# Layer 2's queries moved into the stage of sums, its near heads in one TensorE order, its weight sums in layer 1

## The chip, the cores and the metric

The kernel runs on one core of a Trainium2 chip. The metric is the device time of one execution in microseconds; the median of three runs before the change is 1518.73 us (1516.59 to 1519.83). A profile comes from one more execution, taken with the hardware profiler.

The engines are named as in the profile: PE is TensorE's matmuls, PEld its weight loads, DVE is VectorE, ACT ScalarE, POOL GpSimd, SP SyncE, which issues the DMAs here.

## The reference

A two-layer bidirectional encoder on 1024 tokens of width 1024, with 256 memory tokens. Everything is float32.

```python
h = rmsnorm(x, norm_gain[l])
# layer 1 (even): qa, ka, va, qb, kb, vb, qm, gate = split(h @ w_in_even)
ya = global_gqa(...)          # 8 heads over all tokens
yb = window_gqa(...)          # 8 heads over +-128 tokens
ym = memory_attn(qm, mk, mv)  # 4 heads over the 256 memory tokens
x = x + (concat(ya, yb, ym) * silu(gate)) @ w_out_even
# layer 2 (odd): qc, kc, vc, qm, gate = split(h @ w_in_odd)
yc = neighborhood_attn(qc, kc, vc, rpb_c)   # 16 heads, an 8 x 16 window on the token grid
ym = memory_attn(qm, mk, mv)
x = x + (concat(yc, ym) * silu(gate)) @ w_out_odd
out = rmsnorm(x, final_norm_gain)
```

The change concerns layer 2: 16 near heads (the neighbourhood attention), whose queries, keys and values are 8 tiles of 128 columns of `w_in_odd` each (two heads a tile), 4 memory heads, and 12 tiles of gates.

## The kernel before, in words

**Precision.** Each float32 operand is split in a high and a low part; a product is three matmuls (high x high, high x low, low x high) into one PSUM bank. So a tile of 128 output columns for all 1024 tokens, projected directly, is 8 blocks of the inner dimension x 3 x 2 halves of 512 tokens (`token_steps`, matmul on line 228, or line 59 where `Pinned` issues it).

**Seven products.** Some products are cut in 2 x 2 blocks and formed by seven block products in place of eight, with sums and differences of the blocks (Strassen's scheme in Winograd's form). The output projections of both layers do it (`out_project`); the sums of their weights are made by `weight_sums`, a generator with 16 units, each of a load of a [128, 4, 192] tile, four POOL operations of 128x192 and a store. And `front`, the stage of sums between the layers, does it for pairs of layer 2's input tiles: its loop goes over pairs of tiles, each with seven products of 4 x 3 matmuls (`product`, line 1413), two of which, x and z, are done early for the first five pairs, by a plan written out as a string. The results go to DRAM (`gd` for gates, `mqd` for memory queries) by `end`. Before the change the pairs are gates 8 to 11 and 0 to 5, and the four tiles of memory queries. `front` also makes the values of the first two near pairs.

**Layer 1's heads** (`even`): four `global_pair`s, each of 16 blocks of 128 queries; `side`, the weight sums of layer 1's output, takes one step before each group of two blocks, so 8 steps a pair. Then the windowed heads.

**Layer 2's heads** (`opening`, then `odd`). `opening` computes the memory heads; its TensorE instructions keep the order of the program (`Pinned`), and `fill(SLOT)` puts some 5800 columns of projection work between their parts: the first pair's queries, the values of the other six pairs, the first keys, and second queries. Then `odd` loops over the eight near pairs. `near_head` does one head: for each of 8 blocks of 128 queries the scores (lines 1023, 1024) against up to three neighbouring blocks of keys, on DVE the bias and the maximum (line 1031) and its negation (line 1034), the exponential on ACT (line 1035), the reciprocal on DVE (line 1036) and the scaling on POOL (line 1037); two blocks later the transposes (`flip`, line 122), their split into high and low part (`p_parts`, ACT line 114 and DVE line 462) and the products with the values (line 1006). At each block `pull` takes two steps of work that was put off: the next pair's keys and queries, directly projected, at the end gates 6 and 7 and the first of the output products (`begin_out`, line 1144). `side` makes the sums of layer 2's output weights here, on POOL, two steps a head. Gates 0 to 5 and 8 to 11 are loaded from DRAM and multiplied in `gated`.

`k_pair` evicts a pair of keys on ACT and DVE (line 344) and copies each head's rows to the other 64 partitions by DMA (lines 349, 350). `q_pair` evicts queries by two ACT and two DVE instructions a half (lines 326, 327).

**What sets the order.** The Tile framework simulates the program and orders each engine's instructions by it; `with self.ahead(kind)` moves instructions forward by an offset out of the table `AHEAD`; `issue_after` holds one back behind another; `keep_in_program_order` (`Pinned`) fixes the order of those that it wraps. Layer 2's row of the table:

```python
"l1": dict(first=300, sink=300, evict=300, exp=200, flip=-20, part=200, pv=-60, close=60),
```

Tiles come out of pools with a number of buffers for each name; a new tile waits until the oldest of its name is released.

## Time and profile before

| | |
|---|---|
| median of 3 runs | 1518.73 us |
| the profiled execution | 1515.65 us, its span 1513.9 us |
| granted TensorE clock, mean | 0.994 |
| layer 1's heads, about | 150 to 660 us |
| layer 1's output projection | 660 to 790 us |
| stage of sums (`front`) | 790 to 952 us |
| opening of layer 2 | 952 to 1077 us |
| near heads | 1077 to 1387 us |
| layer 2's output projection | 1387 to 1514 us |

The stages run into each other; the bounds are read from the lines that run in each.

How to read it: the page's first part has busy time, share of the span and number of instructions of each engine; the chain is the work that ended last, followed back from the last instruction. Groups of instructions name the line, the engine, the operation, the tiles (out<-in), the shapes, the count, busy us and mean ns, and then the engine's idle time before them with what ended it. A matmul's duration covers its passage through the array; the spacing of successive starts is what it costs in a stream. In the wait view each row has who waited, for whom, the us in total, the times, and the longest.

### The profile page before, as it was taken

How to read it: one execution, taken by the hardware profiler on the slowest of the kernel's cores; microseconds unless marked ns; L12 is line 12 of the kernel's file. 1: busy time of each engine (PE TensorE's matmuls, PEld its weight loads, DVE VectorE, ACT ScalarE, POOL GpSimd, SP SyncE). 2: the span in 40 equal slices, each digit the busy share in tenths (PEclk: the TensorE clock that was granted, in tenths of full speed). 3: DMA queues.
4: the chain of work that ended last, by engine and by line, in shares of the span. 5: the costliest groups of instructions: out<-in, count | busy, mean ns of one | idle time of the engine just before them, and what ended most of it. 6: DMA issues, size and time to landing. Idle time of an engine off the chain costs nothing.

```text
span 1513.9 us, 25309 instructions
## 1 busy us (share of the span) xinstructions
PE 1479.4 (98%) x8413; PEld 1281.5 (85%) x8413; DVE 1046.0 (69%) x2255; ACT 830.2 (55%) x1822; POOL 659.9 (44%) x782
## 2 busy tenths in 40 slices
PE   9999999999999999999999999999999999999997
PEld 8898898988888788787878778999788888888886
DVE  7686777767776588777578865443577777777754
ACT  8743665556655365655445544433566666666552
POOL 1323547456563545443450000131456566664355
PEclk9999999999999999999999999999999999999998
DMA  8866323233232423287652434765656666668834
GB/s 300 283 164 183 93 80 125 84 110 101 98 112 79 131 67 112 82 281 255 208 181 94 143 113 162 243 200 166 200 165 185 183 206 206 215 206 300 296 121 137
DMA packets 165794, 252.49 MB, mean 167 GB/s; under 512 B 14752, under 2 KB 95904, under 8 KB 164640
## 3 DMA queue, kind: packets, MB, share of 16 engines
q1 hardware_dynamic: 165232, 250.80, 51.5%
q8 instruction: 66, 1.08, 0.3%
q14 instruction: 64, 0.52, 0.1%
q10 hardware_dynamic: 432, 0.09, 0.0%
HBM read 164.32 MB, written 74.45 MB: 158 GB/s over the span
## 4 chain that ended last, share of the span: by engine, by line
PE 86%; DMA 4%; DVE 4%; ACT 2%; issue 1%; POOL 1%; SPq 0%; POOLq 0%; ACTq 0%; DVEq 0%
PE pj L228 27%; PE tr L122 8%; PE pj L59 6%; PE pv L967 4%; PE pj L1170 4%; PE sa L1170 4%; PE x L1413 3%; PE pv L1006 3%; PE pj L756 3%; PE tr L1170 3%; PE s L1170 2%; PE sa L934 2%; PE sa L935 2%; PE y L1413 2%; PE pv L1170 2%; PE pv L1413 1%
## 5 line engine op out<-in xcount | busy, mean ns | idle before, releaser
L228 PE MATMUL pj<-H,wh 128*128 128x512 f32 x1198 | 397.2, 412 | 0.6 <-DVE vt L299 0.2
L114 ACT ACTIVATE ph<-tr 128x512 fp32r<-128x512 f32 (+2 forms) x336 | 180.2, 541 | 142.4 <-PE tr L122 117.6
L462 DVE TENSOR_TENSOR pl<-tr,ph 128x512 fp32r<-128x512 f32 (+2 forms) x336 | 205.3, 615 | 53.8 <-ACT ph L114 51.7
L228 PE MATMUL pj<-H,wl 128*128 128x512 f32 x599 | 235.8, 394 | 0.0
L228 PEld LDWEIGHTS pj<-H,wh 128*128 128x128 f32 x1198 | 205.3, 189 | 30.3 <-issue 0.8
L144 POOL TENSOR_SCALAR wh<-wraw 128x512 fp32r<-128x512 f32 x78 | 51.8, 665 | 278.8 <-PE x L1413 156.9
L114 ACT ACTIVATE wh<-wraw 128x384 fp32r<-128x384 f32 (+1 forms) x162 | 88.8, 554 | 101.1 <-PE tr L1170 12.4
L228 PEld LDWEIGHTS pj<-H,wl 128*128 128x128 f32 x599 | 112.5, 188 | 26.2
L146 POOL TENSOR_TENSOR wl<-wraw,wh 128x512 fp32r<-128x512 f32 x82 | 108.4, 1323 | 28.6 <-ACT wh L114 24.3
L122 PE MATMUL tr<-ident,P 128*128 128x128 f32 x752 | 115.2, 273 | 1.4 <-POOL P L640 0.7
L1124 POOL TENSOR_TENSOR wl<-wraw,wh 128x384 fp32r<-128x384 f32 x56 | 62.4, 1116 | 114.4 <-ACT wh L114 105.0
L942 POOL TENSOR_SCALAR P<-P,st 128x1024 f32<-128x1024 f32 x64 | 76.6, 1199 | 68.1 <-DVE st L941 68.1
L1037 POOL TENSOR_SCALAR pn<-pn,st 128x384 f32<-128x384 f32 (+1 forms) x128 | 73.4, 577 | 68.1 <-DVE st L1036 40.7
L122 PEld LDWEIGHTS tr<-ident,P 128*128 128x128 f32 x752 | 88.7, 140 | 10.0 <-DVE pl L462 2.2
L940 ACT ACTIVATE P<-sa,st 128x1024 f32<-128x1024 f32 x64 | 71.6, 1119 | 44.1 <-DVE st L939 24.1
L1035 ACT ACTIVATE pn<-pn,st 128x384 f32<-128x384 f32 (+1 forms) x128 | 75.3, 588 | 35.5 <-DVE st L1034 27.5
L939 DVE TENSOR_REDUCE st<-sa 128x1 f32<-128x1024 f32 x64 | 77.7, 1219 | 13.2 <-PE sa L935 10.6
L756 PE MATMUL pj<-ah,H 128*128 128x256 f32 x384 | 73.7, 289 | 1.0 <-DVE H L701 0.9
L1124 DVE TENSOR_TENSOR wl<-wraw,wh 128x384 fp32r<-128x384 f32 (+1 forms) x64 | 46.6, 729 | 32.8 <-ACT wh L114 32.3
L967 PE MATMUL pv<-ph,va 128*128 128x256 f32 x256 | 66.6, 285 | 0.0
L967 PE MATMUL pv<-pl,va 128*128 128x256 f32 x256 | 65.8, 284 | 0.0
L1031 DVE CUSTOM_DVE_ANT_0 pn<-s,bm 128x384 f32<-128x384 f32 x96 | 53.1, 555 | 18.2 <-PE tr L122 12.9
(493 smaller groups left out, 3922.7 us busy)
## 6 DMA issues: line engine op xcount, KB each, us to landing
wraw<-w_o SPq DMA_DIRECT2D x62, 256.0 KB, 3.7
y<-yb SPq DMA_DIRECT2D x24, 512.0 KB, 3.4
wraw<-s SPq DMA_DIRECT2D x64, 192.0 KB, 3.2
y<-sg SPq DMA_DIRECT2D x23, 512.0 KB, 3.6
wraw<-w_e SPq DMA_DIRECT2D x44, 256.0 KB, 3.0
k<-k SPq DMA_DIRECT2D x42, 256.0 KB, 4.8
wraw<-w_mem SPq DMA_DIRECT2D x32, 256.0 KB, 4.3
v<-v SPq DMA_DIRECT2D x8, 1024.0 KB, 4.8
```

The source lines that it names most:

```text
L59: return lambda *a, **k: self.tc.keep_in_program_order(getattr(self.engine, name)(*a, **k))
L114: return self.nc.scalar.activation(out, in_, AF.Copy, scale=scale)
L122: self.turned = self.fence = self.pe.transpose(o, i, self.ident)
L146: e.tensor_tensor(lf, raw, hf, op=OP.subtract)
L228: self.pe.matmul(a[:, :n], s[:, kt % UNIT, :], m, start=(kt == 0 and i == 0), stop=(kt == KT - 1 and i == 2))
L462: nc.vector.tensor_tensor(pl[:, :n], tr[:, :n], ph[:, :n], op=OP.subtract)
L756: self.last = nc.tensor.matmul(a[:, b * 256:(b + 1) * 256], x[kt][:, t], w, start=(kt + b + i == 0), stop=(kt == KT - 1 and i == 2), skip_ ...
L939: nc.vector.tensor_reduce(st[:, 0:1], s, axis=AX.X, op=OP.max, negate=True)
L967: nc.tensor.matmul(o[:, :256], v[:, c + k, kv, :], part[:, k * 256:(k + 1) * 256], start=(c + k == 0 and part is parts[0]), stop=(c + k == ...
L1124: engine.tensor_tensor(lf, raw, hf, op=OP.subtract)
L1170: last = nc.tensor.matmul(bank, s[:, k, :], y[3 * u + k][m][:, cols], start=start and u + k + e == 0, stop=u == 1 and k + e == 4, skip_gro ...
L1413: self.last = nc.tensor.matmul(bank, ws[s][:, k, :], b[k][m], start=start and k + i == 0, stop=k == UNIT - 1 and i == 2, skip_group_check= ...
```

## The change

Five things:

1. Layer 2's eight query tiles go into the stage of sums, in four pairs (`pairs`); the pair of gates 4 and 5 leaves it. `end` evicts queries by one ACT and one DVE instruction a half and stores them to `qd`; the near heads load them (`load_q`).
2. Gates 4 to 7 are projected directly (`gate_out`) and stored to `gd`: gate 6 at the start of the opening, where the first queries were, gates 4, 5 and 7 among the near heads.
3. `near_head` becomes `near`, one stream of 128 blocks over all 16 heads, with TensorE in program order: in step n the transposes of block n-4, the scores of block n, the value products of block n-5, and `fill(STEP)`, 1990 columns of the projections still to be done (keys 1 to 7, gates 4, 5, 7, the begun output products). The negation on DVE goes: the reduction makes minus the score and the minimum. Weights of the next tile are loaded and split in steps behind POOL's scaling (`jobs_of`), and the gating is cut in steps (`gated_steps`).
4. The sums of layer 2's output weights are made in layer 1's global heads: `side` becomes both generators in a chain, one step after each block's scores, twice as many.
5. Buffers: `pn` 6 to 7, `ph` and `pl` 4 to 3, `vt` 2 to 3, `mk` goes out of the list; `SLOT` 5800 to 5500. `k_pair` takes its tiles when the first half is evicted, and not before.

```diff
-SLOT = 5800
+SLOT = 5500
+STEP = 1990
...
+    def gate_out(self, w, nt, dst, cols=((0, 512), (512, 512))):
+        nc = self.nc
+        def sink(p, c, n):
+            t = self.st("vt", [128, 512])
+            nc.scalar.activation(t, p, AF.Tanh, scale=0.5)
+            nc.vector.scalar_tensor_tensor(t, t, 1.0, p, op0=OP.add, op1=OP.mult)
+            nc.sync.dma_start(dst[:, c:c + n], t)
+        return self.token_steps(w, nt, lambda kt, c, n: tuple(t[kt][:, c:c + n] for t in self.h), list(cols), sink)
+
+    def jobs_of(self, w, nt):
+        nc = self.nc
+        raws = [self.wload(w[nt, :, u * UNIT * 128:(u + 1) * UNIT * 128]) for u in range(KT // UNIT)]
+        self.ready[nt] = parts = [[self.st(t, [128, UNIT, 128], F32R, pool=self.base, bufs=4) for t in ("wh", "wl")] for _ in raws]
+        def run():
+            for raw, p in zip(raws, parts):
+                h, l = (t.rearrange("p a b -> p (a b)") for t in p)
+                nc.gpsimd.tensor_scalar(h, raw, 1.0, 1.0, op0=OP.mult, op1=OP.mult)
+                yield
+                nc.gpsimd.tensor_tensor(l, raw, h, op=OP.subtract)
+                yield
...
                 self.normal = nc.gpsimd.tensor_scalar(pt, pt, st[:, 2:3], 0.5, op0=OP.mult, op1=OP.mult)
             pts[i, g, b] = pt
+            with self.tc.issue_after(self.normal.ins):
+                next(side, None)
...
-                with self.tc.issue_after(self.normal.ins):
-                    next(side, None)
...
+    def near(self, made, load_q, load_v, gate, yd, fill):
...
-                nc.tensor.matmul(s[:, :n], qb, kh[:, lo * 128:hi * 128], start=True, stop=False)
-                self.fence = nc.tensor.matmul(s[:, :n], qb, kl[:, lo * 128:hi * 128], start=False, stop=True)
+            self.pe.matmul(s[:, :w], qb, kh[:, lo * 128:hi * 128], start=True, stop=False)
+            self.pe.matmul(s[:, :w], qb, kl[:, lo * 128:hi * 128], start=False, stop=True)
...
-                                               op0=OP.add, op1=OP.max, scale=1.0, scalar=NEG, accum_out=st[:, 0:1])
-                nc.vector.tensor_scalar(st[:, 1:2], st[:, 0:1], -1.0, None, op0=OP.mult)
-                nc.scalar.activation(o, o, AF.Exp, bias=st[:, 1:2], accum_out=st[:, 2:3])
+                                               op0=OP.add, op1=OP.min, scale=-1.0, scalar=-NEG, accum_out=st[:, 0:1])
+                nc.scalar.activation(o, o, AF.Exp, bias=st[:, 0:1], scale=-1.0, accum_out=st[:, 2:3])
...
+            for jobs in (self.jobs, self.later_jobs):
+                with self.tc.issue_after(normal.ins):
+                    while jobs and next(jobs[0], self) is self:
+                        jobs.popleft()
+                    if jobs:
+                        break
...
+        for n in range(128 + 5):
+            if 4 <= n < 132:
+                parts[n - 4] = flips(n - 4)
+            if n < 128:
...
+                scores(n)
...
+                if j < 7 and at == 2:
+                    pair["q"] = load_q(j + 1)
+                if j < 7 and at == 5:
+                    pair["v"] = load_v(j + 1)
...
+                if n == 117:
+                    made["first"]()
+                if at == 0 and j or n == 124:
+                    k = j - (at == 0)
+                    pair[k]["g"] = gate(k, "mk" if k == 7 else "sg")
+            if n >= 5:
+                values(n - 5)
+                if (n - 5) % 16 == 15:
+                    j = (n - 5) // 16
+                    self.later_jobs.append(self.gated_steps(pair[j]["g"], pair[j]["y"], yd, ROWS.index(j)))
+            fill(n)
...
-            else:
-                for i in range(2):
-                    s, r = slice(64 * i, 64 * i + 64), slice(64 - 64 * i, 128 - 64 * i)
-                    self.copy(o[s, i, :], p[s], 0.125)
-                    nc.vector.scalar_tensor_tensor(o[r, i, :], p[s], 0.125, o[s, i, :], op0=OP.mult, op1=OP.subtract)
-            nc.sync.dma_start(dst[:, :, c].rearrange("i p n -> p i n"), o.bitcast(F32))
+            self.copy(o[:, 0, :], p, 0.125)
+            nc.vector.scalar_tensor_tensor(o[:, 1, :], p, 0.125, o[:, 0, :], op0=OP.mult, op1=OP.subtract)
+            for i in range(2):
+                nc.sync.dma_start(dst[i].rearrange("(e p) n -> p e n", e=2)[:, :, c], o[64 * i:64 * i + 64].bitcast(F32))
...
-                pairs = [(O_G + g, O_G + g + 1) for g in (8, 10, 0, 2, 4)] + [(O_QM, O_QM + 1), (O_QM + 2, O_QM + 3)]
+                pairs = [(O_G + g, O_G + g + 1) for g in (8, 10, 0, 2)] + [(n, n + 1) for n in (O_Q, O_QM, O_QM + 2, O_Q + 2, O_Q + 4, O_Q + 6)]
...
-                self.front(wo, pairs, (0, 1, 2, 5, 6, 3, 4), v2, "x.x.V2V2V2V1V2V2V2V1x2z2V2V2V2V1V2V2V2V1x2z2x2z2z2z2", x1, rows1, dests)
+                self.front(wo, pairs, (0, 1, 2, 5, 6, 3, 4, 7, 8, 9), v2, "x.x.V2V2V2V1V2V2V2V1x2z2V2V2V2V1V2V2V2V1x2z2x2z2z2z2", x1, rows1, dests)
...
-        side = self.weight_sums(self.io["w_oe"], sd, "bias", nc.gpsimd)
+        side = chain(*(self.weight_sums(self.io[k], d, "bias", nc.gpsimd) for k, d in (("w_oe", sd), ("w_oo", sd2))))
...
+            todo = [(O_K + 1, keys(1)), (O_K + 2, keys(2)), half(4, 0), (O_K + 3, keys(3)), half(4, 512), (O_K + 4, keys(4)),
+                    (O_K + 5, keys(5)), half(5, 0), (O_K + 6, keys(6)), half(5, 512), (O_K + 7, keys(7)),
+                    (O_G + 7, self.gate_out(w, O_G + 7, gd[7]))]
...
+            made["first"]()
+            yield from begin
...
+        self.near(made, load_q, load_v, gate, yd, lambda n: fill(STEP))
```

`half` is one half of 512 columns of `gate_out`; `begin` is `begin_out`, its matmuls now in program order too.

More of the change, by code (lines that the diff above doesn't have):

```diff
@@ L2 @@
 from contextlib import ExitStack, contextmanager, nullcontext
+from itertools import chain
 import concourse.bass as bass
@@ L351, in k_pair @@
         self.tokens(w, nt, sink)
[L352 removed]
+        return ks
     def v_pair(self, w, nt, natural=False):
@@ new lines, in flips, with values @@
+        def flips(n):
+            h, j = divmod(n, 8)
+            b0, b1 = span(j)
+            tr = self.ps("tr")
+            self.flip((tr[:, (b - b0) * 128:(b - b0 + 1) * 128], pts[8 * h + b][:, (j - b + 1) * 128:(j - b + 2) * 128])
+                      for b in range(b0, b1))
+            return self.p_parts(tr, (b1 - b0) * 128)
+        def values(n):
+            h, j = divmod(n, 8)
+            b0, b1 = span(j)
+            if j == 0:
+                acc[h] = [self.ps("pv") for _ in range(2)]
+            v = pair[h // 2]["v"]
+            for part in parts[n]:
+                for a in range(2):
+                    lo, hi = max(b0, 4 * a), min(b1, 4 * a + 4)
+                    if lo < hi:
+                        self.pe.matmul(acc[h][a][:, (lo - 4 * a) * 128:(hi - 4 * a) * 128], v[:, j, h % 2, :],
+                                       part[:, (lo - b0) * 128:(hi - b0) * 128],
+                                       start=(part is parts[n][0] and j == (0, 3)[a]),
+                                       stop=(part is parts[n][1] and j == (4, 7)[a]), skip_group_check=True)
+            if j in (4, 7):
+                close(h, j // 5)
@@ L1131, in begin_out, with parts @@
     def begin_out(self, w, first, banks, n=1):
-        nc = self.nc
+        def parts(i, u):
+            with self.ahead("w"):
+                raw = self.st("wraw", [128, UNIT * 128], pool=self.base, bufs=4)[:, :384]
+                self.nc.sync.dma_start(raw, w[i][:, u * 384:u * 384 + 384])
+                return self.w_parts(raw, self.either())
+        ws = deque(parts(0, u) for u in range(2))
+        yield 0
         for i in range(n):
```

251 lines of the change are left out of this document (135 added, 116 removed).

## The prediction

> **What bounds the kernel now.** I read the page first, then busy time by stage, then what TensorE waited for.
>
> ```profile
> span 1513.9 us, 25309 instructions
> PE 1479.4 (98%) x8413; PEld 1281.5 (85%) x8413; DVE 1046.0 (69%) x2255; ACT 830.2 (55%) x1822; POOL 659.9 (44%) x782
> PE 86%; DMA 4%; DVE 4%; ACT 2%; issue 1%; POOL 1%; SPq 0%; POOLq 0%; ACTq 0%; DVEq 0%
> ```
>
> TensorE (PE) is busy 98% of the span and holds 86% of the chain that ended last. A busy share doesn't say that every product is needed, so I go by stage. The columns are: length; busy time of PE, weight load, DVE, ACT, POOL; granted clock; share of the DMA engines; GB/s. The rows are layer 1's global heads, its windowed heads, the stage of sums, the opening of layer 2, three pairs of near heads, and a late stretch of them.
>
> ```profile
> 152.00:490.00 338.00, 338.00 (x2052) 297.08 (x2052) 242.90 (x381) 204.34 (x404) 184.33 (x212) 1.00 0.30 96
> 530.00:605.60 75.60, 75.06 (x433) 65.52 (x432) 64.13 (x164) 44.85 (x119) 39.76 (x52) 1.00 0.27 90
> 860.00:952.00 92.00, 91.23 (x395) 73.66 (x394) 57.45 (x91) 38.97 (x68) 3.85 (x4) 1.00 0.43 143
> 952.00:1077.00 125.00, 123.19 (x888) 115.53 (x888) 53.82 (x101) 52.20 (x136) 32.07 (x47) 1.00 0.65 213
> 1135.40:1249.00 113.60, 113.60 (x637) 99.25 (x637) 84.96 (x281) 73.28 (x182) 68.66 (x100) 1.00 0.63 191
> 1362.50:1400.40 37.90, 37.90 (x196) 32.27 (x196) 29.87 (x61) 23.18 (x50) 17.21 (x19) 1.00 0.90 301
> ```
>
> In every stage that the change touches, PE has next to no idle time, at full clock, and no other engine is above 85%. So a product taken away shortens the time by its own length, and an order without old waits can win little. The wait view of PE gives that little, for 952 to 1400 us (layer 2's heads) and then for 832 to 952 us (the sums):
>
> ```profile
> PE pv L59 <- ACT ph L114: 1.3, 1, 1.3
> PE s L1023 <- DMA k<-k: 0.8, 1, 0.8
> PE s L1024 <- DMA k<-k: 0.7, 2, 0.5
> PE tr L122 <- POOL pn L1037: 0.6, 1, 0.6
> PE pv L59 <- DVE pl L462: 0.5, 1, 0.5
> ```
>
> ```profile
> PE x L1413 <- ACT P L114: 2.1, 1, 2.1
> PE x L1413 <- ACT wh L114: 0.5, 1, 0.5
> PE pv L1413 <- DVE t L59: 0.5, 2, 0.3
> PE x L1413 <- DVE P L1445: 0.3, 1, 0.3
> ```
>
> That is 3.9 us in all of layer 2's heads, 2.1 of them (rows 2 to 4) where the near heads begin, and 3.4 us in the sums.
>
> **The change part by part.**
>
> *Products.* From the chain in order of time, a projection in layer 2 and a product in the sums:
>
> ```profile
> 952.44 10.99 PE pj L59 x48
> 902.44 2.75 PE x L1413 x12
> ```
>
> 48 matmuls of 512 columns take 10.99 us, 12 take 2.75 us: 229 ns each in both places. A tile of 128 outputs projected directly is 8 blocks of the inner dimension x 3 terms of the split x 2 column halves = 48 matmuls. A pair of tiles by seven products is 7 x 4 x 3 = 84 in place of 96. Eight query tiles leave the head stages (-384) and come into the sums as four pairs (+336). The pair of gates 4 and 5 leaves the sums (-84); both become direct tiles (+96). Net -36 matmuls, three pairs' saving: 36 x 0.229 = **-8.2 us**. Gates 6 and 7, all keys, values, scores, transposes and the begun output products keep their matmuls; they only change places.
>
> [...]
>
> *Three more pairs in the sums.* They add 252 x 0.229 = 57.7 us there (in the net above) and, with them, that stage's idle time. In the row 860 to 952 us it is 0.77 of 92 us, so 0.5 us more; if each new pair brought a wait like the one of 2.1 us, 6.3. I take **+1.0**, near the row. The query evictions are one ACT and one DVE instruction a half and two stores. DVE is at 62% there, and the stored queries are first read some 60 us later or more, so both are hidden.
>
> *Old waits.* The copies of key rows between partitions (k<-k) made PE wait 0.8 + 0.7 us, the first normalisation 0.6. After the change, the first keys end 12288 columns (5.5 us of products), the last two memory slots and five chunks of the next keys before the first near score. That covers the eviction and the copy (4.8 us, in a row below). I take **-2.0**; the ends are 0 and all five waits, -3.9.
>
> *Weight sums into layer 1.* POOL there, from the groups of 152 to 490 us:
>
> ```profile
> L942 POOL TENSOR_SCALAR P<-P,st 128x1024 f32<-128x1024 f32 x64 | 76.6, 1199 | 68.1 <-DVE st L941 68.1
> L1107 POOL TENSOR_TENSOR bias<-bias 128x192 f32<-128x192 f32 x16 | 10.6, 663 | 0.9
> L1109 POOL TENSOR_TENSOR bias<-bias 128x192 f32<-128x192 f32 x16 | 10.0, 625 | 1.0
> L1106 POOL TENSOR_TENSOR bias<-bias 128x192 f32<-128x192 f32 x16 | 9.7, 604 | 2.9 <-DMA bias<-w_oe 2.9
> L1108 POOL TENSOR_TENSOR bias<-bias 128x192 f32<-128x192 f32 x16 | 9.6, 598 | 0.9
> ```
>
> Sixteen units of 2.5 us become 32: +39.9 us, POOL from 184 to 224 of 338 us (66%). The 32 loads and 32 stores go with them, on SP's queue past the weight loads, into one buffer, so a load now waits for the store just before. DMA is at 0.30 there. PE has 338.00 of 338.00 with sixteen units, so the nearest row says **0**. Without that cover a unit can hold a normalisation, and the transposes behind it, for 2.5 us: 16 x 2.5 = 40 at the far end, which I hold unlikely, since a score comes only every 4 us or so.
>
> *The near heads in a fixed order.* Rows of the groups from 1135.4 to 1249 us, 48 blocks of three head pairs:
>
> ```profile
> L228 PE MATMUL pj<-H,wh 128*128 128x512 f32 x192 | 63.4, 410 | 0.0
> L228 PE MATMUL pj<-H,wl 128*128 128x512 f32 x96 | 37.8, 394 | 0.0
> L1031 DVE CUSTOM_DVE_ANT_0 pn<-s,bm 128x384 f32<-128x384 f32 x36 | 20.0, 556 | 4.2 <-PE tr L122 2.4 <-PE s L1024 0.8
> L462 DVE TENSOR_TENSOR pl<-tr,ph 128x384 fp32r<-128x384 f32 x36 | 19.9, 554 | 2.9 <-ACT ph L114 2.7
> L114 ACT ACTIVATE ph<-tr 128x384 fp32r<-128x384 f32 x36 | 17.6, 488 | 17.4 <-PE tr L122 17.3
> L344 DVE TENSOR_TENSOR k<-pj,k 64x512 fp32r<-64x512 f32 x12 | 8.2, 685 | 1.5 <-ACT k L114 1.3
> L1034 DVE TENSOR_SCALAR st<-st 128x1 f32<-128x1 f32 x48 | 7.0, 147 | 0.4
> L327 DVE SCALAR_TENSOR_TENSOR q<-pj,q 64x512 fp32r<-64x512 f32 x6 | 4.2, 693 | 0.1
> L326 DVE SCALAR_TENSOR_TENSOR q<-pj,q 64x512 fp32r<-64x512 f32 x6 | 4.1, 685 | 10.7 <-ACT q L114 10.7
> ```
>
> And a key copy in the DMA issues of that window (count, size, us to landing):
>
> ```profile
> k<-k SPq DMA_DIRECT2D x12, 256.0 KB, 4.8
> ```
>
> 288 projection matmuls take 288 x 0.229 = 66.0 us; the other 47.6 us are 0.99 us a block. A step now carries 1990 columns of other work, 1990 / 512 x 0.229 = 0.89 us, so a step is 1.88 us where a block took 2.37. DVE loses the negation (7.0 us at most, it overlaps others) and the query evictions (8.3) and gains about 2 us of gates: 84.96 becomes 71.7 of 48 x 1.88 = 90 us, 79%. ACT and POOL lose query work too, POOL the sums. DMA moves less in a shorter time: 24 transfers of the sums and 6 query weights go, 6 query loads come, near 0.7 of the engines; the last window had 0.90 with PE full. So PE stays the bound, and the stage shrinks by what leaves it.
>
> The new risk is the wait of a value product for its transposed block: PE's order is written down, so all later scores, transposes and projections stand behind it. Nearest rows: the windowed heads, DVE at 85%, PE idle 0.54 of 75.6 us (0.7%); the opening, where PE's order is already fixed, 1.81 of 125 (1.4%). For 129 steps x 1.88 = 242 us these give 1.7 and 3.5; I take **+2.5**. The filler ends near step 129, so the last four steps have none. Output products that aren't in the fixed order can stand in: 0, and 4 us if not. The tightest keys (the last pair's) end about 4.7 steps, 8.8 us, before they are read; that covers eviction and copy.
>
> Sum: -8.2 + 1.0 - 2.0 + 0 + 2.5 = **-6.7 us**. The profiled execution took 1515.65 us (span 1513.9); that makes 1509.0. The median of the runs, 1518.73, is 3.1 above the profiled execution, so I predict **1512.0**.
>
> **The rivals.**
>
> *Slower: the fixed order turns DVE's bursts into PE stalls.* Two rows of PE's timeline (start, length) give a score's matmul its spacing, 0.17 us:
>
> ```profile
> 1184.46 0.33 PE L1024 MATMUL s<-k,q 128*128 128x384 f32 x1
> 1184.63 0.34 PE L1006 MATMUL pv<-ph,v 128*128 128x384 f32 x1
> ```
>
> Between the end of a block's transposes and its value products lie a step (1.88 us) and two such matmuls, 2.2 us; the copy on ACT (0.488) and the subtraction on DVE (0.554) need 1.04, so some 1.2 us are free. A key eviction is 2 x 0.685 us on DVE, and the table of priorities puts it (sink, 300) ahead of the parts (200); with one 0.556 of a score before it, that is 1.93 us, a stall of 0.7. Evictions, closes and gating make some 76 such bursts. If they cost 0.15 us a step on the mean, 128 x 0.15 = 19 in place of 2.5: +10, **1529**. It decides from (6.7 + 2.5) / 128 = 0.07 us a step. For it: a DVE near 80% in an order that can't yield. Against: the windowed heads at 85% lose 0.7%. Chance 0.16.
>
> *More gain: nothing new is late.* All of layer 2's waits go (-3.9) with nothing in their place: -8.2 - 3.9 = -12.1, **1506.6**. For it: scores, transposes and values lie three to five steps apart. Against: DVE's higher share. Chance 0.20.
>
> *The change doesn't save what it says: the sums pay.* The three new pairs need their own weights split before their first product, as the wait on wh (0.5) shows; if each waits 2.1, +6.3, the fixed order keeps its 2.5 and the old waits stay: -8.2 + 6.3 + 2.5 = +0.6, **1519**. Against: in 92 us of that stage PE idled 0.77. Chance 0.10.
>
> **How the numbers follow.** Forecast 0.54. From 1502 to 1522 the range holds the forecast with its ends, the larger gain and the sums' case, 0.84 together, and leaves out the slower rival. A measurement tells about 0.2%, 3 us, from no change. Faster by more: 0.20 and 0.50 of the forecast, 0.70. Same: 0.10 and 0.04, 0.14. Slower: 0.16.
>
> **What would show it.** PE's instructions fall by 36. The sums grow by some 58 us, and layer 2's heads shrink by some 66. In the near stage DVE stands near 80% and PE idles about 1%; the wait on k<-k is gone. The global heads still show PE without idle time. It is wrong if PE waits there on POOL's normalisation, in the near stage on pl for more than 9 us together, or if the new pairs in the sums wait.

## The result and the profile after

The changed kernel takes 1537.28 us (median of 4 runs, 1534.86 to 1538.08), the kernel before, timed beside it, 1517.99 (1516.59 to 1519.83): the ratio is 1.0124 [1.0106, 1.0141]. It is 19.3 us slower. The prediction said 1512.0 us, 1502 to 1522. Each experiment below was timed beside the kernel before, too, whose median was between 1517.99 and 1520.30 us; its ratio is to that, and times of different runs compare only within such a spread.

The head of the page of the changed kernel, and its chain:

```profile
span 1536.3 us, 25337 instructions
PE 1482.3 (96%) x8377; PEld 1275.3 (83%) x8377; DVE 1052.0 (68%) x2164; ACT 836.5 (54%) x1839; POOL 642.9 (42%) x766
PE 71%; DMA 12%; DVE 6%; POOL 4%; issue 3%; ACT 2%; SPq 2%; POOLq 0%; DVEq 0%; ACTq 0%
```

TensorE (PE) has 36 instructions less, as it should, and yet 2.9 us more busy time; its share of the span fell from 98% to 96%, and its share of the chain from 86% to 71%, while DMA's rose from 4% to 12% and DVE's from 4% to 6%. To find the stage, I cut both traces at the same marks: the first product of the sums, the first of the opening, the first and the last transpose of a near block, the first product behind the heads that reads `H` for the scores' banks. Busy time by stage of the kernel before (sums, opening, near heads, the stretch behind their last transpose); columns as in the prediction:

```profile
784.60:952.30 167.70, 162.00 (x794) 134.18 (x793) 118.94 (x202) 78.04 (x138) 6.34 (x6) 1.00 0.41 138
952.30:1086.50 134.20, 132.03 (x929) 122.40 (x928) 58.09 (x115) 54.68 (x143) 35.06 (x51) 1.00 0.63 204
1086.50:1386.80 300.30, 298.38 (x1664) 258.81 (x1663) 223.08 (x738) 196.27 (x484) 185.74 (x264) 1.00 0.66 204
1386.80:1422.80 36.00, 36.00 (x161) 29.66 (x160) 26.39 (x36) 18.29 (x36) 13.30 (x11) 1.00 0.90 308
```

The same four of the changed kernel:

```profile
790.90:1018.60 227.70, 221.37 (x1045) 182.68 (x1044) 155.63 (x259) 103.86 (x183) 6.32 (x6) 0.99 0.46 144
1018.60:1150.20 131.60, 129.92 (x923) 121.28 (x922) 59.66 (x114) 55.17 (x145) 31.92 (x48) 1.00 0.71 232
1150.20:1414.60 264.40, 251.51 (x1436) 214.76 (x1434) 199.46 (x602) 184.24 (x466) 139.55 (x191) 0.99 0.71 227
1414.60:1444.10 29.50, 26.02 (x110) 21.02 (x109) 17.21 (x25) 11.98 (x23) 10.10 (x8) 0.94 0.63 205
```

The sums grew by 60.0 us, near the 58.7 predicted. The opening, the near heads and the stretch behind them shrank by 2.6, 35.9 and 6.5, 45.0 in all, where 65.5 were predicted. So some 20 us are missing in layer 2's heads, and PE, which had 1.9 us without work in the old near stage, now has 12.9. The stages ahead of the sums end 6.3 us later (790.9 against 784.6), and the output projection is 1.1 us longer (92.2 against 91.1). What PE waited for in the near stage and the stretch behind it:

```profile
PE pv L61 <- DVE pl L526: 9.9, 10, 3.6
PE pv L61 <- ACT ph L116: 4.1, 2, 3.3
PE tr L61 <- POOL pn L1083: 1.5, 1, 1.5
```

The old waits on `k<-k` are gone. In their place stand value products (`pv`) that wait for the two parts of their transposed block, the low one on DVE above all. Two stretches of the timeline show why `pl` is late. First the longest wait; DVE:

```profile
1316.92 0.56 DVE L526 TENSOR_TENSOR pl<-tr,ph 128x384 fp32r<-128x384 f32 x1
1317.39 0.67 DVE L1122 TENSOR_TENSOR yb<-pv,bt 64x512 f32<-64x512 f32 x1
1320.63 0.69 DVE L464 TENSOR_TENSOR yb<-yb,sg 128x512 f32<-128x512 f32 x1 [2.57 <-DMA sg<-g]
1321.24 0.69 DVE L466 TENSOR_TENSOR yb<-yb,sg 128x512 f32<-128x512 f32 x1
...
1322.38 0.55 DVE L526 TENSOR_TENSOR pl<-tr,ph 128x384 fp32r<-128x384 f32 x1
```

and PE beside it:

```profile
1319.08 0.34 PE L61 MATMUL pv<-ph,v 128*128 128x384 f32 x1
1322.99 0.69 PE L61 MATMUL pv<-pl,v 128*128 128x384 f32 x1 [3.57 <-DVE pl L526]
1323.47 1.05 PE L61 MATMUL pj<-H,wh 128*128 128x512 f32 x2
1324.33 0.63 PE L61 MATMUL pj<-H,wl 128*128 128x512 f32 x1
1324.76 1.05 PE L61 MATMUL pj<-H,wh 128*128 128x512 f32 x2
...
1326.95 0.62 PE L61 MATMUL pj<-H,wh 128*128 128x512 f32 x2
1327.41 0.39 PE L61 MATMUL pj<-H,wl 128*128 128x512 f32 x1
```

The transposes of this block ended about 1316.9, 2.2 us before its first value product. DVE stood still from 1318.06: at the head of its queue was the gating of the pair before (`yb<-yb,sg`), and that waited 2.57 us for the load of the gates. Gates 0 to 6 share one buffer, so a load starts when the pair before has let it go. Here the load stands in the program at the start of the next pair, waited 1.5 us for the store out of the buffer, was issued at 1313.85 and landed nearly 7 us later. Behind the gating stood its second half, a reciprocal, a score and then `pl`. PE's order is written down, so the projection that could have filled the gap stood behind the value product. After the wait the next products are 0.43 us apart (1323.47 to 1324.33), and only from 1326.95 on 0.23 again.

Second, the end of the near stage, busy time in three windows of 38 us, early, at the wait just shown, and last:

```profile
1228.00:1266.00 38.00, 37.83 (x224) 32.77 (x223) 29.11 (x93) 27.48 (x71) 21.75 (x31) 1.00 0.64 207
1304.00:1342.00 38.00, 34.31 (x191) 29.56 (x192) 25.26 (x80) 23.30 (x60) 22.01 (x30) 0.96 0.65 199
1380.00:1418.00 38.00, 31.28 (x169) 25.82 (x167) 28.91 (x71) 26.36 (x63) 17.16 (x20) 1.00 0.82 291
```

PE has 0.2 us without work in the first, 3.7 in the second and 6.7 in the last, with DVE at 77%, 66% and 76%: DVE's share doesn't tell them apart. The last window has no gate load in the way; there DVE's queue holds the parts of the output projection's operands:

```profile
1396.20 1.21 DVE L120 TENSOR_TENSOR q<-q 128x512 fp32r<-128x512 f32 x1
1397.34 0.55 DVE L1078 CUSTOM_DVE_ANT_0 pn<-s,bm 128x384 f32<-128x384 f32 x1
...
1397.82 0.41 DVE L526 TENSOR_TENSOR pl<-tr,ph 128x256 fp32r<-128x256 f32 x1
```

and the value product of that block, on PE, starts at 1398.29 after a wait of 2.00 us. Right behind the near stage ACT's queue does the same, and that is the second-longest wait:

```profile
1416.95 0.63 ACT L116 ACTIVATE q<-q 128x512 fp32r<-128x512 f32 x1 [0.40 <-DMA q<-y]
1418.15 0.47 PE L61 MATMUL pv<-ph,v 128*128 128x384 f32 x1 [3.28 <-ACT ph L116]
```

The transposes of this block ended before 1414.5, and their copy `ph` on ACT began at 1417.60. Ahead of it stood the splits of two operands, which waited 0.60 and 0.40 us for their loads, a weight's split and a head's closing copy.

### The profile page after: what moved, and what is told of

Read it like the earlier page. It is cut to its first block, busy times and chain, and to the rows that moved or that the text cites. A ratio compares the mean times of both kernels' runs of the same rounds, so it can differ in the third digit from the quotient of the medians.

```text
span 1536.3 us, 25337 instructions
## 1 busy us (share of the span) xinstructions
PE 1482.3 (96%) x8377; PEld 1275.3 (83%) x8377; DVE 1052.0 (68%) x2164; ACT 836.5 (54%) x1839; POOL 642.9 (42%) x766
## 3 DMA queue, kind: packets, MB, share of 16 engines
q8 instruction: 66, 1.08, 0.3%
## 4 chain that ended last, share of the span: by engine, by line
PE 71%; DMA 12%; DVE 6%; POOL 4%; issue 3%; ACT 2%; SPq 2%; POOLq 0%; DVEq 0%; ACTq 0%
PE pj L230 13%; PE pj L61 11%; PE x L1522 6%; PE tr L124 4%; PE pj L1279 3%; PE pv L1031 3%; PE y L1522 3%; PE pv L61 3%; PE sa L1279 3%; PE s L61 2%; PE tr L1279 2%; PE s L1279 2%; PE pv L1522 2%; PE tr L61 2%; PE pv L1279 2%
## 5 line engine op out<-in xcount | busy, mean ns | idle before, releaser
L230 PE MATMUL pj<-H,wh 128*128 128x512 f32 x704 | 234.4, 414 | 0.6 <-DVE vt L301 0.2
L146 POOL TENSOR_SCALAR wh<-wraw 128x512 fp32r<-128x512 f32 x48 | 31.8, 663 | 261.5 <-PE x L1522 217.0
L230 PE MATMUL pj<-H,wl 128*128 128x512 f32 x352 | 139.0, 395 | 0.0
L230 PEld LDWEIGHTS pj<-H,wh 128*128 128x128 f32 x704 | 120.1, 190 | 18.3 <-issue 0.8
L61 PE MATMUL pj<-H,wh 128*128 128x512 f32 x384 | 121.6, 398 | 0.0
L61 PE MATMUL s<-k,q 128*128 128x384 f32 (+1 forms) x352 | 86.3, 341 | 1.7 <-DMA q<-mq 1.7
L1003 DVE TENSOR_REDUCE st<-sa 128x1 f32<-128x1024 f32 x64 | 77.5, 1218 | 13.3 <-PE sa L999 12.2
L148 POOL TENSOR_TENSOR wl<-wraw,wh 128x512 fp32r<-128x512 f32 x52 | 67.9, 1308 | 28.4 <-ACT wh L116 22.7
L230 PEld LDWEIGHTS pj<-H,wl 128*128 128x128 f32 x352 | 66.3, 188 | 15.4
L61 PE MATMUL pj<-H,wl 128*128 128x512 f32 x192 | 76.0, 396 | 0.0
```

Source lines behind the costliest of these rows:

```text
L61: return lambda *a, **k: self.tc.keep_in_program_order(getattr(self.engine, name)(*a, **k))
L230: self.pe.matmul(a[:, :n], s[:, kt % UNIT, :], m, start=(kt == 0 and i == 0), stop=(kt == KT - 1 and i == 2))
L1003: nc.vector.tensor_reduce(st[:, 0:1], s, axis=AX.X, op=OP.max, negate=True)
```

## The experiments

My theory after this reading: a value product stands one step (two microseconds) behind its transposes, and whatever is ahead of `pl` in DVE's queue, or of `ph` in ACT's, for longer stalls PE. The rivals: the written order itself is the loss; the weight sums in layer 1 are; DVE simply has too much to do.

**One part alone.** The kernel before with only the second weight sums in layer 1:

```diff
-        side = self.weight_sums(self.io["w_oe"], sd, "bias", nc.gpsimd)
+        side = chain(*(self.weight_sums(self.io[k], d, "bias", nc.gpsimd) for k, d in (("w_oe", sd), ("w_oo", sd2))))
...
-        side = self.weight_sums(self.io["w_oo"], sd, "mk", nc.gpsimd)
+        side = iter(())
```

> The kernel before with one part of the change: the second weight sums in layer 1's global heads, one step after each block's scores, and none among the near heads. Theory 1 (the fixed order of the near heads costs the time): as before within 1.5 us, 1516.5 to 1519.5, PE without waits in the global heads. Theory 2 (POOL's doubled sums delay layer 1, since the changed kernel reaches the stage of sums 6.3 us later): 1522 to 1525, with PE waits on POOL's normalisation in the global heads.

Measured: 1521.76 us, 1.0021 [1.0007, 1.0035] of the kernel before. It costs some 3 us and is not where 19 are.

The kernel before with only the queries by seven products in the sums, and the old near heads:

```diff
-                pairs = [(O_G + g, O_G + g + 1) for g in (8, 10, 0, 2, 4)] + [(O_QM, O_QM + 1), (O_QM + 2, O_QM + 3)]
+                pairs = [(O_G + g, O_G + g + 1) for g in (8, 10, 0, 2)] + [(n, n + 1) for n in (O_Q, O_QM, O_QM + 2, O_Q + 2, O_Q + 4, O_Q + 6)]
```

> The kernel before with one part of the change: the queries in the stage of sums, gates 4 and 5 direct in the opening, near heads and weight sums as before. Theories 1 and 2: the 36 matmuls are saved, 1508 to 1512. Theory 3 (the near heads are short of time in any order once the query projections no longer fill it): 1520 or more, with PE waits on the transposed blocks' parts or on POOL in the near stage.

Measured: 1549.55 us, 1.0212 [1.0191, 1.0233]. Without the written order the queries' move loses more, not less. The near heads shrank by 30.2 us only. Two of PE's waits there:

```profile
PE tr L122 <- POOL pn L1048: 10.2, 8, 3.5
PE s L1034 <- DMA k<-k: 4.0, 2, 2.2
```

With the query projections gone, the old stage has 288 of its 747 filler products less, three quarters of what a pair has left (36 of 48) stand in the pair's first half, and the normalisation on POOL is exposed. Spreading it (one filler call in place of two between the parts, for all pairs but the last):

```diff
-                self.near_head(q[i], ks[i], v, i, bm[i], y, side, 2)
+                self.near_head(q[i], ks[i], v, i, bm[i], y, side, 1 if j < 7 else 2)
```

> The queries-only kernel with one step of put-off work a block, in place of two, for the first seven pairs, so that the keys' projections are spread over all 16 blocks of a pair. Theory 4 and 5 both ask for filler in every block: 1549 falls by 15 us or more, to 1515 to 1535. If the filler's spacing does not matter: 1547 to 1552.

Measured: 1584.07 us, 1.0426 [1.0375, 1.0478]. What it waits for:

```profile
PE s L1034 <- DMA k<-k: 32.8, 7, 7.8
```

Spread, the filler makes the next keys too late. With neither spacing does the old stage do without the queries' products; that no order of it could isn't shown.

**Undoing one part.** The changed kernel with the near heads' instructions on PE no longer pinned to the program's order:

```diff
+        self.pe = nc.tensor
```

> The changed kernel with the near heads' TensorE instructions no longer kept in program order; the framework orders them. Theory 1: the near stage loses its waits on pl and ph, 18 us less, 1517 to 1522. Theory 3: the waits stay under other names, 1532 or more.

Measured: 1553.36 us, 1.0241 [1.0212, 1.027], 16 us slower than with the fixed order. That the order is the loss, my first rival, falls. The free order's waits are the same kind:

```profile
PE pv L1110 <- DVE pl L526: 6.6, 15, 1.0
PE pv L1110 <- ACT ph L116: 5.4, 5, 3.2
```

The changed kernel with the second weight sums back in the near heads, a step every fourth block:

```diff
+            if n % 4 == 0:
+                with self.tc.issue_after(normal.ins):
+                    next(self.side, None)
```

> The changed kernel with the second weight sums back among the near heads (a step every fourth block) and layer 1 as before. Theory 2: layer 1 gets its 3 to 6 us back, 1531 to 1534, if the near heads don't pay. Theory 1: 1536 to 1540, since POOL's work comes into the stage that waits.

Measured: 1535.58 us, 1.0123 [1.0098, 1.0147]: the changed kernel's time within the error. In its trace the sums begin 7.1 us earlier than in the changed kernel (783.8), and the near heads take 7.6 us more (272.0).

DVE's negation of a row's maximum back in the near softmax (147 ns, once a block):

```diff
-                                               op0=OP.add, op1=OP.min, scale=-1.0, scalar=-NEG, accum_out=st[:, 0:1])
+                                               op0=OP.add, op1=OP.max, scale=1.0, scalar=NEG, accum_out=st[:, 0:1])
+                nc.vector.tensor_scalar(st[:, 1:2], st[:, 0:1], -1.0, None, op0=OP.mult)
```

> The changed kernel with one thing undone in a near head's softmax: DVE's separate negation of the row maximum (147 ns, 48 in three pairs of heads, 128 in all) is back, so DVE has some 19 us more work in the near stage at most. If DVE's lateness is what TensorE waits for there, each of 128 steps has less slack by up to 0.15 us and the time rises by 3 to 10 us, to 1540 to 1547. If the stage loses for a reason that is not DVE's (the gate load, the normalisation on POOL, the granted clock), the time stays at 1537 within 2 us.

Measured: 1540.57 us, 1.0151 [1.0131, 1.0171]; 3.3 us more than the changed kernel, in the direction of the theory, but the intervals touch. So 19 us more on DVE cost some 3 (6 in the near heads of its trace): the amount of DVE's work is a small part at most, and a run below has the same work without the loss.

**What `pl` waits behind.** The gates loaded at their own pair's eighth block, into two buffers by turns; those of pairs 5 and 7 (counted from 0) are loaded where they were, into the second buffer:

```diff
-                if at == 0 and j or n == 124:
+                if at == 8 and j not in (5, 7) or n in (96, 124):
...
-                    pair[k]["g"] = gate(k, "mk" if k == 7 else "sg")
+                    pair[k]["g"] = gate(k, "mk" if k % 2 else "sg")
```

> The changed kernel with the near pairs' gates loaded into two buffers in turn and, but for 5 and 7, half a pair earlier, so that the gating on DVE finds them. Theory 4a (a gating multiplication that waits for its load holds up DVE's queue, and the value products behind it): the two waits of 3.6 and 1.3 us go, 1531 to 1533, and the near stage gets 4 to 6 us shorter. Theory 5 (the steps are too short for DVE anyway): the waits move to other blocks, 1536 to 1538.

Measured: 1535.39 us, 1.0111 [1.0087, 1.0135]: 2 us, hardly more than the error. Of the changed kernel's three waits of the gating, those of pairs 3 and 4 (1.30 and 2.57 us) are gone; that of pair 5, whose load isn't made earlier, is 3.17 us in place of 1.42, and PE waits 2.35 us behind it. The waits for `pl` sum to 9.1 us still, in 11 places, and those for `ph` to 6.7.

One of the output projection's seven sets of operands, the second, held on ACT behind the last block's copy:

```diff
-        y = self.y_parts(yd, tags["y"][1], "t1")
+        with self.tc.issue_after(self.copies[-1].ins) if last else nullcontext():
+            y = self.y_parts(yd, tags["y"][1], "t1")
```

> The changed kernel with the splits of the output projection's second set of operands held on ACT behind the last copy of a transposed block. Theory 4b (these splits stand ahead of the last blocks' parts on ACT and DVE): the waits of the last 40 us of the near heads go, some 5 us, 1531 to 1533. Theory 5: 1536 to 1538, or slower where the output projection then waits for its operands.

Measured: 1537.89 us, 1.0123 [1.0096, 1.015]: no gain. The wait of 2.00 us behind `q<-q` isn't in its trace, but other operands (`H<-H`, `k<-k`) still stand ahead of `pl` and `ph`: one split on ACT waited 3.59 us for its load, and PE 2.58 us for `ph` behind it. The near stage with the stretch behind it takes 295.4 us (265.0 and 30.4) against 293.9. The output projection behind is 3.7 us longer than in the changed kernel.

The value products a step later, block n-6 in step n where it was n-5 (the loads' places move with it):

```diff
-            if n >= 5:
-                values(n - 5)
+            if n >= 6:
+                values(n - 6)
```

> The changed kernel with a block's value products two steps behind its transposes in place of one. Theory 4c (the value products stand too close behind the split on ACT and DVE): the waits on pl and ph all but go, 10 to 15 us, 1522 to 1528. Theory 5 (DVE or ACT fall behind as a whole): the waits go to the transposes or the scores, 1534 or more.

Measured: 1525.32 us (ten runs, 1517.65 to 1533.32), 1.0036 [1.0012, 1.006]. One step of distance is worth 12 us (13 by the ratios). No value product waits any more in its trace; what is left are transposes behind `pl` (3.4 us), `st` on DVE (2.9) and `pn` (2.1). Two of the longest have a load at the head of a queue in front of them: the gating on DVE waited 3.95 us for its load, and PE 2.35 behind it; an operand's split on ACT waited 3.40, and PE 2.70 behind it. The profiled execution took 1533.3 us, the longest of the ten, so I use its kinds of waits only.

**Both, and the weight sums apart.** Values later and gates early together:

```diff
+                values(n - 6)
...
+                    pair[k]["g"] = gate(k, "mk" if k % 2 else "sg")
```

> The changed kernel with two edits in the near heads: the value products a step later and the gates' weights loaded early; the second weight sums stay in layer 1. The run with both and the sums ahead of layer 2 had the heads of layer 2 shorter by 64.8 us, as the prediction said (65.5), but 14 us more in the sums. If the terms add up: sums +59, heads -65, layer 1 +3 to +6: 1515 to 1519, level with the kernel before within 0.3 %. If the near heads only came out well there by the weight sums being elsewhere, the time is near the 1525 of the run with the value products later alone.

Measured: 1513.40 us (nine runs, 1509.96 to 1517.26) against 1518.42 of the kernel before: 0.9968 [0.9956, 0.998], faster by 5 us, and 24 less than the changed kernel. Sums, opening, near heads and the stretch behind them, and the waits in the last three:

```profile
788.50:1016.50 228.00, 221.25 (x1046) 182.65 (x1045) 155.64 (x259) 103.89 (x183) 6.34 (x6) 0.99 0.46 144
1016.50:1147.80 131.30, 129.82 (x922) 121.23 (x921) 59.49 (x114) 55.20 (x145) 31.91 (x48) 1.00 0.72 237
1147.80:1394.90 247.10, 244.06 (x1434) 213.21 (x1433) 201.37 (x602) 184.33 (x467) 140.66 (x192) 1.00 0.76 239
1394.90:1419.60 24.70, 24.70 (x111) 20.16 (x110) 16.23 (x24) 11.33 (x22) 9.84 (x8) 1.00 0.78 256
```

```profile
PE tr L61 <- DVE st L1082: 1.4, 1, 1.4
PE tr L61 <- POOL pn L1083: 0.7, 2, 0.5
PE tr L61 <- DVE pl L526: 0.5, 1, 0.5
PE s L61 <- DMA k<-k: 0.4, 1, 0.4
```

The same DVE work (201 us), more densely packed (81% of the stage), and PE idles 3.0 us of 247, 1.2%. The near stage and the stretch behind it are 17.3 and 4.8 us shorter than in the changed kernel: 13.3 us less time without work (12.9 and 3.5 against 3.0 and 0.0) and 8.8 less busy time for the same products (251.51 and 26.02 against 244.06 and 24.70). Of the second part, up to 3.4 us are, by my estimate, two slow stretches behind the two longest waits: the mean granted clock is 0.76 from 1320 to 1327 us and 0.83 from 1414 to 1424, so 0.24 x 7 and 0.17 x 10 = 1.7 us each, and products of 512 columns start 0.43 us apart in both where 0.23 is usual; the rest I put down to the end of the product ahead of each wait, which counts as busy (0.34 us where its spacing is 0.17), but that isn't measured by itself.

The same with PE's order not pinned:

> The run with values later and gates early (1513.4), with one thing undone: TensorE's order in the near heads is not pinned, as in the run with 1553, so the planner may place the value products and the filler as it likes. If the written order is worth its 16 us whatever the slack, 1529. If the missing slack of the value products is what cost the order its gain, and a free order finds its own slack, the two are level, 1513 to 1517, and the prediction's worry about an order that can't yield was idle. If a free order loses more because it is the planner's costs that place the value products (and the loop's distance is ignored), over 1535.

Measured: 1538.5 us, 1.0137 [1.0115, 1.016]. The written order is worth 25 us with the longer distance, 16 with the short one: the last of the three cases.

The second weight sums a third time, into the stage of sums, where POOL works 6 us of 228; 24 units of 128 columns in the weights' own buffers:

```diff
+                self.side = self.weight_sums(io["w_oo"], sd[1], "wraw", nc.gpsimd)
...
             product(y, unit(s1), t1)
+            with tc.issue_after(self.last.ins):
+                next(self.side, None)
```

> The changed kernel with the second weight sums moved once more: not into layer 1, but into the stage of sums before layer 2, on the GpSimd that is idle there, in 24 units of 128 columns with a tile of their own; layer 1 is as in the kernel before. If the sums cost what the marks of layer 1 show (3.2 us to the first windowed head, 6.3 to the first product of the sums), the time is 3 to 6 us under the changed kernel's, 1531 to 1534, and the mark of the first windowed head is back within 1 us of the kernel before. If those marks differ by chance alone, the time is the changed kernel's, 1537. If the 24 units hold something in the sums (their loads and stores stand on the same queue as the query stores), that stage grows by more than 60 us.

Measured: 1550.74 us, 1.0227 [1.0204, 1.0249], 13 us slower than the changed kernel: the third case. The stage is 240.3 us. DVE's groups in it, here and then in the changed kernel:

```profile
L1228 DVE TENSOR_TENSOR wl<-wq,wh 128x512 fp32r<-128x512 f32 x46 | 35.5, 780 | 10.4 <-ACT wh L116 9.4 <-PE x L1522 0.9
L1570 DVE TENSOR_TENSOR wq<-wq,wq 128x512 f32<-128x512 f32 x17 | 14.7, 867 | 0.2
...
L1547 DVE TENSOR_TENSOR P<-P,x 128x512 f32<-128x512 f32 x13 | 8.5, 677 | 0.0
```

```profile
L1228 DVE TENSOR_TENSOR wl<-wq,wh 128x512 fp32r<-128x512 f32 x46 | 31.5, 688 | 34.2 <-ACT wh L116 24.7 <-PE x L1522 9.0
L1570 DVE TENSOR_TENSOR wq<-wq,wq 128x512 f32<-128x512 f32 x17 | 11.7, 688 | 0.2
L1547 DVE TENSOR_TENSOR P<-P,x 128x512 f32<-128x512 f32 x13 | 8.5, 682 | 0.0
```

The two largest groups on DVE with both inputs in SBUF take 780 and 867 ns where they took 688, and the one whose second input is in PSUM is unchanged; POOL works only 75 of the 240 us, and a group of 6 with two such inputs (`wraw<-wq,wq`, 868 to 968 us) stays at 692. DVE's busy time rose from 155.6 to 170.6 us, though it had room; but every weight passes through it on its way to PE. The units also take the buffers that the stage's own weights use, so how much of the 13 us belongs to which isn't told apart.

With values later, gates early and the sums there:

> Three edits together: the value products a step later (as in the run with 1525 us), the gate loads early, and the second weight sums in the stage of sums. If the terms add up, 1525 less 3 to 6 for the weight sums less 1 to 2 for the gates: 1517 to 1521, level with the kernel before, and the near stage idles under 1.5 %. If the value products' lateness and the gates' lateness are the same time counted twice, 1520 to 1522. If the change's whole account is right but for these terms, it has to come under the kernel before by 3 us or more; a time at or above the kernel before says that another term of the account fails, which I would look for in the last third of the near stage and behind it.

Measured: 1526.78 us, 1.0058 [1.0035, 1.0082]. The heads and what follows are 64.8 us shorter than in the kernel before, as predicted; the sums are 74.2 longer. So the two losses are separate.

The price of the sums in layer 1, by leaving them out; the output projection reads layer 1's sums in their place, so this kernel doesn't compute the reference:

```diff
-                self.out_project(io["w_oo"], sd[1], yd[1], x1d, done, OUT[1], (x, y), first, 2, last=True)
+                self.out_project(io["w_oo"], sd[0], yd[1], x1d, done, OUT[1], (x, y), first, 2, last=True)
```

> As the run with values later and gates early, but the second weight sums are left out: the output projection of layer 2 reads the first layer's sums, so one part of the computation isn't done. It prices the second weight sums: the time of the run beside it less this one is what they cost in layer 1. If the prediction's 0 holds, the two are equal within 2 us; if the marks of layer 1 tell the truth, this one is 3 to 6 us faster, 1511 to 1514, and that less the kernel before, -5 to -8, is what the rest of the change is worth once the value products have their slack, against the predicted -6.7.

Measured: 1513.90 us (ten runs), 0.9963 [0.9948, 0.9978], level with the 1513.40 of the run with them. They cost nothing that these runs can tell, which is some 3 us. The marks of layer 1 that I had read as 3 to 6 us scatter: the sums begin at 783.8 to 788.5 us (785.8 on the mean) in the seven traces without the second weight sums there, and at 785.9 to 794.3 (788.7) in the ten with them. Yet there is a price. In each of those ten traces PE has 0.3 to 3.0 us without work between 152 and 490 us, and in none of the seven. Here this run and then the changed kernel, with a stall in it:

```profile
152.00:490.00 338.00, 338.00 (x2055) 297.14 (x2054) 244.25 (x380) 203.37 (x404) 183.35 (x212) 1.00 0.30 97
```

```profile
152.00:490.00 338.00, 336.11 (x2031) 294.51 (x2030) 241.79 (x376) 201.61 (x400) 221.78 (x276) 0.99 0.41 131
226.65 0.60 POOL L1210 TENSOR_TENSOR bias<-bias 128x192 f32<-128x192 f32 x1 [3.26 <-DMA bias<-w_oe]
232.30 1.24 PE L124 MATMUL tr<-ident,P 128*128 128x128 f32 x3 [1.08 <-POOL P L639]
```

A unit of the sums stood 3.26 us at the head of POOL's queue, waiting for its load, with normalisations behind it, and PE waited 1.08 us for one of them.

And in units half as wide through two buffers; the windowed heads' bias, which has the same tile name, is cut in two for it:

```diff
-        n = 192
+        n = 96
...
-            t = self.st(tag, [128, 4, n])
+            t = self.st(tag, [128, 4, n], bufs=2)
```

> As the run with values later and gates early, but layer 1's weight sums go in units half as wide through two buffers, so that a load no longer waits for the store just before it and GpSimd finds its operands there. If the waits of GpSimd on these loads are what layer 1 lost, the mark of the first windowed head comes back from +3 to within 1 us of the kernel before, and the time is 3 us lower than in the run beside it, 1512 to 1516. If layer 1 loses because GpSimd's work itself lengthens or delays DVE's and GpSimd's other work, nothing is gained, or 1 to 3 us are lost by the doubled number of instructions.

Measured: 1511.38 us (1509.59 to 1516.3), 0.9958 [0.9943, 0.9973]: the fastest of all, by 7 us under the kernel before, but not told apart from the run without this edit.

## Why the prediction was wrong

*Products, -8.2, and three more pairs, +1.0: right.* PE has 36 instructions less, and the sums grew by 60.0 us (60.3 in the run with both edits) for 58.7.

*Old waits, -2.0: in keeping with the runs, not measured by itself.* The wait on `k<-k` went (0.4 us of it is in the run with both edits). In the run with both edits, the opening, the near heads, the stretch behind them and the rest are 2.9, 53.2 and 11.3 us shorter and 0.9 longer than in the kernel before, 66.5 together; 65.5 were predicted, the fixed order's 2.5 among them.

*Weight sums into layer 1, 0: right within the 3 us that can be told, but not as argued.* The term came from a row with PE busy 338.00 of 338.00 us; that row has 336.11 now, and a sign by which the prediction called itself wrong, PE waiting there on POOL's normalisation, is there with 1.08 us. The case that was held unlikely, a unit that holds a normalisation, does occur, but only now and then: the far end, 40 us, never came. Alone in the kernel before, the same edit cost 3.2 us [1.1, 5.3], and there it also changed the near heads; what of that is layer 1's stays open.

*The near heads in a fixed order, +2.5: this step failed.* It measured 24 us more than the run with the longer distance and the early gates, which idles 3.0 us in the near stage, near the 2.5 that were put. The step took its rows from the windowed heads and the opening as the nearest, by DVE's share and by the fixed order. Neither was near in what decides, the distance between a block's transposes and the value products that need them, and what can stand at the head of DVE's queue in that time. The prediction had 1.2 us of slack. It went through the evictions that can use it up, 0.7 us over, and didn't ask the same of two other things that stand in the same queue: the gating, whose load waits for a buffer (2.57 us before the instruction, and its two halves behind), and the operands of the output projection (0.8 to 1.2 us each on DVE, and on ACT with waits for their loads), of which it counted nothing; the 4 us set aside for the last steps were for missing filler. The second of these is read from the timelines alone: holding one set of the operands back gained nothing. Only the DVE time of the gates was counted, about 2 us (the rival "slower" names the gating among its bursts, also by its length alone), and not the wait in front of it: 2.57 us at the head of DVE's queue held the gating's two halves, a reciprocal, a score and `pl`, and PE waited 3.57 us for that `pl`.

*The rival "slower" had the mechanism and nearly the size*: 0.15 us a step assumed, 23.9 / 128 = 0.19 measured; 1529 for 1537. Its chance of 0.16 came from the windowed heads' 0.7%, the same row that misled the forecast. Its name was half wrong, though: the fixed order is not the fault (freeing it costs 16 and 25 us), the distance in it is. And the test that the prediction wrote down, PE waiting on `pl` for more than 9 us, was met with 9.9, where the whole loss is over twice that: a wait view counts neither the slow products behind a wait nor the end of the one before it.

*What isn't settled*: early gates alone gave 2 us, later values alone 12, both 24. The traces say it too: the near heads and the stretch behind them take 293.9 us in the changed kernel, 293.7, 281.9 and 271.8. Part of the reason is seen in them. Early gates alone leave the gate of pair 5 late and everything else that stands ahead of `pl` and `ph`; later values alone leave the wait of 3.95 us for a gate and that of 3.40 us for an operand, which reach PE with 2.35 and 2.70 us. But with both edits the second of these is down to 1.02 us, though the gates' edit moves no operand's load, and why is not shown.

## What to carry to other kernels

Where an engine's order is written by hand, count the slack of each dependent product in microseconds, and set against it the longest run of work, waits included, that can stand ahead of its producer in that engine's queue; a mean share of busy time doesn't tell it (77% and 76% here, with 0.2 and 6.7 us lost). When work is taken out of a stage, what is left has shorter steps, so distances that are counted in steps shrink too. A change that loses may be one distance away from a gain: here one step and an earlier load turned +19 us into -5.

## What the runs showed of the hardware

After PE's wait of 3.57 us, products of 512 columns started 0.43 us apart for three microseconds where 0.23 is usual. In layer 1 of the changed kernel, 14 us (228 to 242) with 1.3 us without work in them show a mean granted clock of 0.88, so 0.12 x 14 = 1.7 us less at full clock, as an estimate; 0.76 over 7 us, behind the wait of 3.57 us, gives 0.24 x 7 = 1.7 too:

```profile
228.00:242.00 14.00, 12.67 (x54) 9.71 (x52) 8.58 (x13) 6.87 (x14) 13.84 (x17) 0.88 0.38 133
1320.00:1327.00 7.00, 4.01 (x14) 3.32 (x15) 3.34 (x11) 1.79 (x5) 4.15 (x6) 0.76 0.77 215
```

In the first stretch four products of 512 columns start 0.43 us apart as well (235.40, 235.83, 236.26 and 236.68), and the two at 237.96 are 0.23 apart again; the pauses of PE there were 1.3 us in all, 1.08 of them in one wait that ended at 232.30. So a lower clock followed a wait of 1.08 us and one of 3.57; what sets it isn't shown.

Two groups of DVE's instructions with two inputs in SBUF became 13% and 26% longer (688 to 780 and 867 ns) in a stage where POOL had 75 us of work in place of 6, and one with an input in PSUM didn't (682 and 677). A group of 6 with two inputs in SBUF stayed at 692 ns, and the DMA engines' share rose in that stage too, from 0.46 to 0.62, so POOL's work as the cause isn't shown by itself. POOL, idle there, was not free room: the stage became 12.6 us longer (240.3 against 227.7), though how much of that the longer instructions on DVE made is open.
